# A hybrid recurrent trunk on one core: the SSD's first token piece moved in between the RWKV key steps

## The chip, the cores and the metric

The kernel runs on one core of a Trainium2 chip. The metric is the device time of one execution in microseconds, the median of three runs.

## The reference

The reference is a trunk of two layers over one sequence of 1024 tokens, 1024 wide, in float32. Layer 0 mixes with gated DeltaNet and GLA, layer 1 (the "odd" one) with Mamba-2 SSD and RWKV-7; a squared-ReLU MLP follows each. Only the odd mixer matters here:

```python
z, xbc, dt_raw, pd = _split(h @ w_in, ODD_SPLITS)      # 512, 1024, 8, 1792 columns
xbc = silu(conv(xbc)); dt = softplus(dt_raw + dt_bias)
yc = ssd_chunked(xs, dt, -exp(a_log), b_in, c_in)
yc = rmsnorm((yc + xs * d_skip) * silu(z))
r, k, v, xw, xa, xg = token_shift_mix(pd)              # split of the last 1792 columns
yd = rwkv7_scan(r, decay, k, v, -kk, kk * a)           # 8 heads, state 64 x 64
yd = (groupnorm(yd) + bonus) * g
return concat([yc, yd]) @ w_out
```

## The kernel before

**Products.** Every projection is made in three matmuls per tile: operands are split into a high and a low part (`whi`, `wlo` of the weights, two `hn` tiles of the activations), and high x high, high x low and low x high are added up. `piece` loads a block of weights with SyncE's queue into `wst`, casts it to `whi` on ScalarE and subtracts on VectorE for `wlo`. `feature_tiles` makes 128 features by 512 tokens (24 matmuls of 128x512 per tile). `token_piece` makes 128 tokens by `width` features, four token tiles per half of the sequence. The piece of z and the time steps dt has width 264 (256 columns of z, 8 of dt): 8 x 24 = 192 matmuls of 128x264.

**What sets the order.** The program is one Python pass that emits instructions; a tile scheduler then places them on the engines by priority. Work beside the projections comes in two ways. Closures that an eviction leaves (`later`) stand in `pend`; they are run at the end of a tile (`run_pending(n)`), or, while `spread` is set, a quarter of them after every second k. Background tasks (`spawn`) advance by `step`; `tick(w)` counts columns in units of 512, and every 7 of these are one step in the odd mixer. A 128x264 matmul counts 264/512.

**The odd mixer.** `odd` projects for two groups of four RWKV heads. For each pair p it makes key and receptance tiles (`keys_receptance(p)`), whose closures compute norms, row factors, Gram products (`grams`, tile `G`) and transposed updates, and then values. After both pairs of a group it flushes the closures, stores N of all 16 chunks to DRAM (`d_Nr`), and `inverse(g)` inverts the triangles of the whole group on VectorE, 60 instructions on tile `NL`, and stores them to `d_Ur`. A chunk of the scan loads these into `hh`. After group 1 (g = 0) the scan is spawned (`rwkv`, class "c", a delay of 16 steps) and `spread` is set. The scan runs 32 chunks in order, 16 of group 1 and 16 of group 2, three steps to a chunk, and each chunk's matmuls come as `T` and `Z` (part of the inverse), `uv`, `w`, `Q` (the state) and `r`. While it runs, the rest of the projections fills TensorE: the keys of group 2 (g = 1), the z piece, the SSD's convolved features (`feats`, whose taps are `cy` and `th` on VectorE) and the second z piece. Chunk 14 waits in the program until `begun` holds group 2, that is until the flush behind its key steps. After that come `posts` (group norm, gating and the store to `d_o`), the SSD scan (`ssd_scan`, eight chunks per group, each stores `y` to `d_o`), and `tail`, which reads `d_o` back (`ol`) and makes the output projection (`wst<-in_odd_w_out`, `pd`).

Group 2's key steps are the loop `for p in (2 * g, 2 * g + 1)` with g = 1; z's evictions are `z_evac(0, True)` (gate to `d_z`, time steps to `dtr`); `scalars()` behind it reads `dtr`.

Of the kernel before, what the change touches and what calls it, by code (L numbers as in the profile page):

```python
# [39 lines left out]
class Trunk:  # L40
# [223 lines left out]
    def token_piece(self, cols, width, hnT, evac, halves=(0, 1), mid=None, w=None):  # L264

        w = w or self.token_weights(cols, width)
        for half in halves:
            if half and mid is not None:
                mid()
            hh, hl = hnT[half]  # L270
            for tt in range(4):
                n = len(self.pend)
                sl = slice(tt * 128, tt * 128 + 128)
                ps = self.pd()[:, 0:width]
                for k in range(8):
                    hi, lo = (t[:, k % 2, :] for t in w[k // 2])
                    for j, (wt, x) in enumerate(((hi, hh), (lo, hh), (hi, hl))):
                        self.mm(ps, x[:, k, sl], wt, k + j == 0, k + j == 9)
                        self.tick(width / 512)
                with self.urgent():  # L280
                    evac(half * 4 + tt, ps)
                self.run_pending(n)
# [734 lines left out]
    def odd(self, hnT, d_o, tail):  # L1017
        nc, io, tc = self.nc, self.io, self.tc
        gp = nc.gpsimd
        W = io["odd_w_in"][0]  # L1020
        with ExitStack() as ctx:
# [183 lines left out]
            def values(p):  # L1205
                def v_evac(half, ps):
                    y = mixed(self.s2("my"), half, ps, 8 + p)

                    def turned():
                        pv = self.transpose4(y)  # L1210
                        vt = self.s2("vt")
                        self.cp(vt, pv)
                        self.store(d_v[half * 512:half * 512 + 512, p * 128:p * 128 + 128].rearrange("(c p) d -> p c d", p=128),
                                   vt.rearrange("p (c d) -> p c d", c=4))
                    self.later(turned)
                self.feature_tile(W, 2568 + p * 128, hnT, v_evac)


            def z_evac(c0, gates):
                def f(t, ps):  # L1220
                    if gates:
                        self.vcp(dtr[:, t, :], ps[:, 256:264])
                    self.gate2(ps[:, 0:256], d_z[t * 128:t * 128 + 128, c0:c0 + 256])
                return f

            def xbc_evac(ft):
                def f(half, ps):
                    y = self.conv_silu2(half, ps, self.s_cw, ft, keep, bias=self.s_cb[:, 0, ft:ft + 1])
                    if ft >= 4:
                        kind, gg = (ft - 4) // 2, ft % 2  # L1230
                        self.store(d_bc[half * 4:half * 4 + 4, :, gg, kind, :].rearrange("c f t -> f c t"), y.rearrange("p (c t) -> p c t", c=4))

                    def turned():
                        pt = self.transpose4(y)
                        xt = self.s2("xt")
                        self.cp(xt, pt)
                        dst = d_x[:, ft * 128:ft * 128 + 128] if ft < 4 else d_b[:, (ft - 4) * 128:(ft - 4) * 128 + 128]
                        self.store(dst[half * 512:half * 512 + 512].rearrange("(c p) d -> p c d", p=128), xt.rearrange("p (c d) -> p c d", c=4))
                    if ft < 6:
                        self.later(turned)  # L1240
                return f
# [8 lines left out]
            def inverse(g):  # L1250
                lane = lambda d: d[g].rearrange("k b q x n -> (k b q x) n")
                self.lanes_inverse(lane(d_N), lane(d_U), 128, P)
# [72 lines left out]
            def rwkv():  # L1325

                order = [(g, c) for g in range(2) for c in range(16)]
                own = [[] for _ in order]
                pres = [pre(g, c, own[16 * g + c]) for g, c in order]

                def ahead(i):
                    if i < 32:
                        next(pres[i])

                ahead(0)
                ahead(1)
                ahead(0)
                for _ in pres[0]:
                    yield
                ahead(1)  # L1340
                for i, (g, c) in enumerate(order):
                    while i == 14 and 1 not in begun:
                        yield
                    ahead(i + 2)
                    parts = [chain(g, c, *own[i])] + pres[i + 1:i + 2]
                    for _ in range(3):
                        for p in parts:
                            next(p, None)
                        yield
                    ahead(i + 2)  # L1350
                    if c % 2:
                        scanned.add((g, c // 2))
# [138 lines left out]
            def posts():  # L1491
                for g in range(2):
                    for t in range(8):
                        while (g, t) not in scanned:
                            yield
                        post_p(g, t)
                        yield

            def feats(*fts):
                for ft in fts:  # L1500
                    self.feature_tile(W, 512 + ft * 128, hnT, xbc_evac(ft))

            for g in range(2):
                for p in (2 * g, 2 * g + 1):
                    keys_receptance(p)
                values(2 * g)
                self.flush()
                inverse(g)
                values(2 * g + 1)
                if g == 0:  # L1510
                    self.spawn(rwkv(), "c", 1, 16)
                    self.spread = True
# [7 lines left out]
            gnb = self.bc_row(post_pool, io["rwkv_gn_b"][0], 512, "gnb")  # L1520
            self.scope(ctx, "p", half=1, ldh=5, sm=5)
            self.spawn(posts(), "p", 4, 12)
            self.token_piece([(W, 0, 256), (W, 1536, 8)], 264, hnT, z_evac(0, True))
            with self.core("s"):
                scalars()
            for g in range(2):
# [593 lines left out]
```

## Time and profile before

| | |
|---|---|
| median of three runs | 2557.88 us (2552.94 to 2570.62) |
| profiled execution | 2559.73 us |
| its span | 2557.9 us |
| mean granted clock of TensorE | 0.986 |
| TensorE (PE) busy | 97% |
| weight loads (PEld) | 81% |
| VectorE (DVE) | 64% |
| ScalarE (ACT) | 44% |
| GpSimd (POOL) | 21% |

The profile is one execution, and its own time is 1.85 us above the median of the runs. The odd mixer's projections of group 2 lie at about 1375 to 1519 us, the z piece at 1520 to 1572, the SSD's features up to about 1730, and the end of the SSD scan with the first products of the output projection at 1789 to 1840.

### The profile page before, as it was taken

What the parts mean: (1) busy time and instruction counts of PE and PEld (TensorE: products, weight loads), DVE (VectorE), ACT (ScalarE), POOL (GpSimd) and SP (SyncE); (2) the same over time, 40 slices, a digit from 0 to 9 for tenths busy, and PEclk for the clock granted to TensorE, in tenths of its full rate; (3) what the DMA queues carried; (4) which work ended last, traced back from release to release, by engine and by line L of the source; (5) the groups of instructions that cost most, each with busy time, mean ns of one, the idle gap of its engine ahead of it and who ended that gap; (6) DMA issues with size and microseconds to landing.
All of it is one profiled execution on the core that took longest, in us unless ns stands there. A gap on an engine that the chain in (4) does not pass through costs nothing. (4 is left out here: it accounts for less than half of the span.)

```text
span 2557.9 us, 39479 instructions
## 1 busy us (share of the span) xinstructions
PE 2491.4 (97%) x14230; PEld 2079.6 (81%) x14230; DVE 1645.1 (64%) x2865; ACT 1135.3 (44%) x2139; POOL 541.4 (21%) x546
## 2 busy tenths in 40 slices
PE   7999999999999999999999999999899999999998
PEld 6788898997777788888777788888897778788887
DVE  6677443446587765668366558777657677757476
ACT  5732344336544454333443333444536544533343
POOL 2020123301344300001032202344212443200001
PEclk9999999999999999999999799999999999999999
DMA  4556545644766677566235356666645766677474
GB/s 143 152 152 190 160 140 165 222 141 153 218 231 221 227 268 262 202 254 207 91 112 163 118 161 190 192 187 203 221 149 174 228 217 232 210 275 281 175 265 150
DMA packets 447908, 492.59 MB, mean 193 GB/s; under 512 B 56177, under 2 KB 302178, under 8 KB 447714
## 3 DMA queue, kind: packets, MB, share of 16 engines
q1 hardware_dynamic: 447714, 490.08, 59.3%
q8 instruction: 113, 1.85, 0.3%
q14 instruction: 81, 0.66, 0.1%
HBM read 344.69 MB, written 145.28 MB: 192 GB/s over the span
## 5 line engine op out<-in xcount | busy, mean ns | idle before, releaser
L162 PE MATMUL pd<-hn,whi 128*128 128x512 f32 x1216 | 413.5, 414 | 1.2 <-DVE cy L185 1.1
L162 PE MATMUL pd<-whi,hn 128*128 128x256 f32 (+2 forms) x2048 | 394.0, 288 | 9.4 <-ACT hn L169 4.1
L162 PEld LDWEIGHTS pd<-whi,hn 128*128 128x128 f32 x2048 | 321.8, 190 | 15.5 <-ACT hn L172 4.4
L162 PE MATMUL pd<-wlo,hn 128*128 128x256 f32 (+2 forms) x1024 | 294.9, 288 | 0.6 <-DVE f L182 0.3
L162 PEld LDWEIGHTS pd<-hn,whi 128*128 128x128 f32 x1216 | 225.9, 191 | 54.9 <-issue 8.0
L1864 PE MATMUL pm<-hn,hn 128*128 128x512 f32 x1152 | 263.3, 389 | 0.0
L1864 PEld LDWEIGHTS pm<-hn,hn 128*128 128x128 f32 x1152 | 216.1, 188 | 45.6 <-DVE x L178 0.6
L162 PE MATMUL pd<-hn,wlo 128*128 128x512 f32 x608 | 249.4, 410 | 0.2 <-DVE wlo L178 0.2
L172 ACT CAST hn<-sr 128x1024 fp32r<-128x1024 f32 x104 | 108.9, 1047 | 268.4 <-PE pm L1864 99.3
L178 DVE TENSOR_TENSOR hn<-sr,hn 128x1024 fp32r<-128x1024 f32 x104 | 128.0, 1231 | 113.8 <-ACT hn L172 113.3
L162 PEld LDWEIGHTS pd<-wlo,hn 128*128 128x128 f32 x1024 | 194.4, 190 | 2.7 <-DVE wlo L178 1.2
L189 POOL TENSOR_TENSOR rs<-rs,mhalf 128x1 f32<-128x1 f32 x40 | 24.4, 610 | 769.8 <-DVE rs L178 519.0
L178 DVE TENSOR_TENSOR wlo<-wst,whi 128x512 fp32r<-128x512 f32 (+2 forms) x172 | 125.8, 736 | 90.8 <-ACT whi L172 83.9
L172 ACT CAST whi<-wst 128x512 fp32r<-128x512 f32 (+2 forms) x172 | 106.4, 620 | 175.1 <-PE pd L162 127.5
L1864 PE MATMUL pd<-hn,hn 128*128 128x512 f32 x720 | 182.7, 389 | 0.0
L1864 PE MATMUL pt<-hn,hn 128*128 128x512 f32 x720 | 182.7, 389 | 0.0
L1551 PE MATMUL pm<-rf,whi 128*128 128x512 f32 x512 | 162.8, 399 | 11.0 <-DVE h L178 10.9
L1551 PE MATMUL pm<-hn,whi 128*128 128x512 f32 x512 | 162.4, 398 | 1.8 <-ACT whi L172 1.2
L1864 PEld LDWEIGHTS pt<-hn,hn 128*128 128x128 f32 x720 | 135.1, 188 | 28.1
L1864 PEld LDWEIGHTS pd<-hn,hn 128*128 128x128 f32 x720 | 135.1, 188 | 28.1
L162 PEld LDWEIGHTS pd<-hn,wlo 128*128 128x128 f32 x608 | 116.1, 191 | 25.9 <-issue 1.6
L1551 PEld LDWEIGHTS pm<-rf,whi 128*128 128x128 f32 x512 | 96.9, 191 | 37.0 <-issue 10.3
(439 smaller groups left out, 4922.8 us busy)
## 6 DMA issues: line engine op xcount, KB each, us to landing
w<-in_mlp_w_dram SPq DMA_DIRECT2D x140, 512.0 KB
sr<-d_s SPq DMA_DIRECT2D x104, 512.0 KB
hh<-in_mlp_w_dram SPq DMA_DIRECT2D x64, 512.0 KB
d_s<-s SPq DMA_DIRECT2D x128, 256.0 KB
d_s<-x SPq DMA_DIRECT2D x64, 256.0 KB
hh<-d_rec SPq DMA_DIRECT2D x32, 512.0 KB
wst<-in_even_w_in_dram SPq DMA_DIRECT2D x56, 256.0 KB
wst<-in_odd_w_in_dram SPq DMA_DIRECT2D x52, 256.0 KB
```

The lines of the kernel that those rows point to most:

```text
L162: self.nc.tensor.matmul(out=out, lhsT=lhsT, rhs=rhs, start=start, stop=stop)
L172: self.nc.scalar.copy(out=out, in_=in_)
L178: (eng or self.nc.vector).tensor_tensor(out=out, in0=a, in1=b, op=op)
L189: self.nc.gpsimd.tensor_tensor(out=out, in0=in_, in1=self.mhalf.broadcast_to(list(in_.shape)), op=ALU.pow)
L1551: self.nc.tensor.matmul(out=ps, lhsT=wt[l][:, k, sl], rhs=x[r][:, k, :], start=start and k + j == 0, stop=k + j == n + 1, skip_group_check ...
L1864: self.nc.tensor.matmul(out=ps[tt], lhsT=l[x][:, k, sl], rhs=r[y][:, k, :], start=new and b + k + q == 0, stop=k + q == 5, skip_group_chec ...
```

## The change

The z piece moves from behind the flush of group 2 to between its key steps: tokens of the first half ahead of `keys_receptance(2)`, tokens of the second half ahead of `keys_receptance(3)`. Each call loads and splits the piece's weights itself. `token_piece` gets the spreading of closures that `feature_tiles` has. Nothing else is different.

```diff
@@ token_piece
                 n = len(self.pend)
+                each = -(-n // 4) if self.spread else 0
                 sl = slice(tt * 128, tt * 128 + 128)
                 ps = self.pd()[:, 0:width]
                 for k in range(8):
...
                         self.tick(width / 512)
+                    if k % 2:
+                        now = min(n, each)
+                        self.run_pending(now)
+                        n -= now
                 with self.urgent():
                     evac(half * 4 + tt, ps)
                 self.run_pending(n)
@@ odd
+            def z_early(half):
+                self.token_piece([(W, 0, 256), (W, 1536, 8)], 264, hnT, z_evac(0, True), halves=(half,))
+
             for g in range(2):
                 for p in (2 * g, 2 * g + 1):
+                    if g:
+                        z_early(p - 2)
                     keys_receptance(p)
...
             self.spawn(posts(), "p", 4, 12)
-            self.token_piece([(W, 0, 256), (W, 1536, 8)], 264, hnT, z_evac(0, True))
             with self.core("s"):
                 scalars()
```

**TensorE at the scan's start.** The scan's first chunks stand among the first matmuls of group 2. `pd` is the projection's accumulator, `pm` the scan's. Before, they stand among matmuls of 128x512:

```order
L162 MATMUL pd_2316_13451<-hn_1983_11772,whi_2260_13221 128x512
L162 MATMUL pm_2279_13286<-T_2277_13283,hh_2273_13271 32x32 x4
L162 MATMUL pd_2316_13451<-hn_1984_11773,whi_2260_13221 128x512
L162 MATMUL pd_2316_13451<-hn_1983_11772,wlo_2261_13222 128x512
L162 MATMUL pd_2316_13451<-hn_1983_11772,whi_2260_13221 128x512
L162 MATMUL pm_2289_13320<-hh_2273_13271,Z_2278_13284 32x32 x4
L162 MATMUL pm_2293_13349<-uv_2274_13275,hh_2273_13271 64x64 x4
```

and in the changed kernel among the z matmuls of 128x264:

```order
L162 MATMUL pm_2286_13378<-T_2282_13369,hh_2264_13295 32x32 x4
L162 MATMUL pd_2308_13456<-whi_2303_13445,hn_1983_11772 128x264
L162 MATMUL pd_2308_13456<-wlo_2304_13446,hn_1983_11772 128x264
L162 MATMUL pd_2308_13456<-whi_2303_13445,hn_1984_11773 128x264
L162 MATMUL pd_2308_13456<-whi_2306_13452,hn_1983_11772 128x264
L162 MATMUL pm_2291_13402<-w_2281_13363,hh_2262_13289 64x64 x4
L162 MATMUL pm_2292_13408<-hh_2264_13295,Z_2283_13370 32x32 x4
```

The z piece now lies here, and the key steps of group 2 lie later in the scan by as many steps.

**SyncE where the scan reaches group 2.** `d_Ur<-NL` stores the inverse of group 2; `hh_2654` before and `hh_2652` after are the loads of chunk 16, its first chunk. Before, the store stands here, with group 1's loads behind it and chunk 16's load 25 rows behind the store (not in this piece):

```order
L157 DMA d_Ur_11854<-NL_2458_14100 128x1024
L157 DMA d_z_11850<-th_2574_14772 128x256
L157 DMA d_y_11847<-w_2555_14647 64x256
L157 DMA uv_2579_14788<-d_rv_11845 64x256
L157 DMA hh_2601_14910<-d_Ur_11854 32x4x32
```

In the changed kernel:

```order
L157 DMA d_Ur_11854<-NL_2560_14644 128x1024
L157 DMA wst_3022_16664<-in_odd_w_in_dram 128x4x128
L157 DMA pg_2785_15694<-d_g_11846 128x256
L157 DMA d_o1_11837<-py_2739_15521 128x256
L157 DMA hh_2652_15129<-d_Ur_11854 32x4x32 x2
L157 DMA hh_2677_15237<-d_Ur_11854 32x4x32 x2
L157 DMA hh_2695_15325<-d_Ur_11854 32x4x32 x2
```

The loads of chunks 16, 17 and 18 have moved up to the store.

**SyncE in the tail.** `wst<-in_odd_w_out` are the weights of the output projection, `d_o1<-y` the stores of the SSD chunks (`y_3406` chunk 6, `y_3428` chunk 7 of the second SSD group in the changed kernel). Before, the weights stand here, far ahead of the last chunks:

```order
L157 DMA hh_3453_18395<-d_h_95 128x1024
L157 DMA wst_3456_18401<-in_odd_w_out_dram 128x2x256
L157 DMA wst_3459_18407<-in_odd_w_out_dram 128x2x256
L157 DMA wst_3462_18413<-in_odd_w_out_dram 128x2x256
L157 DMA d_y_11847<-w_3144_17135 64x256
L157 DMA d_o1_11837<-y_3093_16938 128x256
L157 DMA wst_3465_18419<-in_odd_w_out_dram 128x2x256
```

In the changed kernel:

```order
L157 DMA d_o1_11837<-y_3406_18194 128x256
L157 DMA ol_3445_18331<-d_o1_11837 128x512
L157 DMA ol_3446_18333<-d_o1_11837 128x512
L157 DMA wst_3468_18429<-in_odd_w_out_dram 128x2x256
L157 DMA ol_3453_18351<-d_o1_11837 128x512
L157 DMA ol_3454_18353<-d_o1_11837 128x512
L157 DMA d_o1_11837<-y_3428_18255 128x256
L157 DMA wst_3471_18435<-in_odd_w_out_dram 128x2x256
L157 DMA wst_3474_18441<-in_odd_w_out_dram 128x2x256
L157 DMA wst_3477_18447<-in_odd_w_out_dram 128x2x256
```

The projection's loads have moved behind the stores of the last two chunks. On TensorE in the same place, the projection's first matmuls (`pd_3468` before, `pd_3480` after) stood among the SSD chunks' small ones (`xdt,E`, `bc`, `xdd,sb`, `sS,bc`; `ident,ol` are the tail's transposes):

```order
L162 MATMUL pm_3348_18005<-xdt_3324_17889,E_3308_17811 128x64 x4
L162 MATMUL pm_3358_18036<-bc_3329_17928 128x128
L162 MATMUL pd_3468_18425<-whi_3457_18403,hn_3294_17746 128x256
L162 MATMUL pd_3468_18425<-wlo_3458_18404,hn_3294_17746 128x256
L162 MATMUL pm_3360_18041<-xdd_3326_17891,sb_3307_17807 128x256
L162 MATMUL pm_3362_18046<-sS_3336_17950,bc_3305_17805 128x256
```

In the changed kernel the first of them has 30 rows of small matmuls right ahead of it, of which these are the last:

```order
L162 MATMUL pm_3444_18325<-xdt_3427_18254,E_3413_18209 128x64 x4
L162 MATMUL pm_3447_18335<-sS_3435_18286,bc_3410_18203 128x256
L166 MATMUL pm_3455_18355<-ident_78,ol_3445_18331 128x128 x4
L166 MATMUL pm_3456_18368<-ident_78,ol_3446_18333 128x128 x4
L162 MATMUL pd_3480_18453<-whi_3469_18431,hn_3292_17726 128x256
```

They have moved from among the chunks to behind the last one.

## Rows read from the trace of the kernel before

**Rows 1.** The page's first lines: span; busy time, share and instructions of each engine.

```profile
span 2557.9 us, 39479 instructions
PE 2491.4 (97%) x14230; PEld 2079.6 (81%) x14230; DVE 1645.1 (64%) x2865; ACT 1135.3 (44%) x2139; POOL 541.4 (21%) x546
```

**Rows 2.** Windows: stretch and length, busy time per engine, granted clock, DMA share, GB/s.

```profile
core 0: us, PE busy (x) PEld busy (x) DVE busy (x) ACT busy (x) POOL busy (x), PEclk, DMA share, GB/s
1424.50:1434.70 10.20, 10.20 (x68) 8.43 (x65) 1.95 (x5) 2.87 (x8) 0.00 (x0) 0.50 0.15 52
1451.80:1472.30 20.50, 20.50 (x77) 15.83 (x77) 7.51 (x14) 4.31 (x9) 5.01 (x4) 0.50 0.30 92
1503.00:1509.80 6.80, 6.80 (x28) 5.81 (x27) 0.04 (x1) 1.57 (x4) 1.34 (x1) 0.50 0.60 193
1519.80:1572.00 52.20, 52.20 (x496) 46.84 (x494) 42.22 (x138) 17.36 (x47) 7.08 (x10) 1.00 0.62 179
1793.10:1800.00 6.90, 4.47 (x15) 3.85 (x16) 5.22 (x14) 5.74 (x19) 4.19 (x7) 0.51 0.58 183
```

**Rows 3.** Timeline of PE: wide matmuls at full clock, then at the lower one.

```profile
start us, us, engine line op out<-in xcount [idle before <-releaser]
1391.04 0.63 PE L162 MATMUL pd<-hn,whi 128*128 128x512 f32 x2
1391.50 0.40 PE L162 MATMUL pd<-hn,wlo 128*128 128x512 f32 x1
1455.45 1.05 PE L162 MATMUL pd<-hn,whi 128*128 128x512 f32 x2
1456.31 0.63 PE L162 MATMUL pd<-hn,wlo 128*128 128x512 f32 x1
```

**Rows 4.** Timeline of PE: the matmuls of one scan chunk, between wide ones.

```profile
1483.32 0.68 PE L162 MATMUL pm<-r,hh 64*64 64x64 f32 x8
1484.29 1.16 PE L162 MATMUL pt<-ar,bk 64*128 64x128 f32 x16
...
1488.41 1.82 PE L162 MATMUL pm<-uv,hh 128*128 128x128 f32 x20
1490.16 0.50 PE L162 MATMUL pd<-hn,whi 128*128 128x512 f32 x1
...
1492.79 0.61 PE L162 MATMUL pm<-Q,hh 128*128 128x128 f32 x4
1493.69 0.50 PE L162 MATMUL pd<-hn,wlo 128*128 128x512 f32 x1
```

**Rows 5.** Timeline of PE: matmuls of the z piece.

```profile
1526.94 0.41 PE L162 MATMUL pd<-whi,hn 128*128 128x264 f32 x2
1527.18 0.28 PE L162 MATMUL pd<-wlo,hn 128*128 128x264 f32 x1
```

**Rows 6.** Lines by form: z weights' splits (1490 to 1545), conv taps (1572 to 1700).

```profile
L178 DVE TENSOR_TENSOR wlo<-wst,whi 128x528 fp32r<-128x528 f32 x2 | 1.4, 709 | 1.3 <-ACT whi L172 1.3
L172 ACT CAST whi<-wst 128x528 fp32r<-128x528 f32 x2 | 1.3, 634 | 0.9 <-PE pd L162 0.9
L185 DVE SCALAR_TENSOR_TENSOR cy<-pd,cols,cy 128x511 f32<-128x511 f32 x11 | 8.2, 742 | 3.1 <-ACT cy L169 3.1
```

**Rows 7.** Tile NL, 1500 to 1600 (count, ns min/median/max, first and last start).

```profile
L178 DVE TENSOR_TENSOR tl<-NL x30: 185/337/543, 1519.6 to 1557.7; 128x30 f32<-128x30 f32 x2, 128x58 f32<-128x58 f32 x2, 128x84 f32<-128x84 f32 x2, 128x108 f32<-128x108 f32 x2
L178 DVE TENSOR_TENSOR NL<-NL,tl x30: 166/345/620, 1520.1 to 1558.4; 128x30 f32<-128x30 f32 x2, 128x58 f32<-128x58 f32 x2, 128x84 f32<-128x84 f32 x2, 128x108 f32<-128x108 f32 x2
L157 SPq DMA_DIRECT2D d_Ur<-NL x1: 320/320/320, 1558.7 to 1558.7; - x1
```

**Rows 8.** Timeline of SyncE's queue: chunk 16's loads of the inverse.

```profile
1579.66 0.80 SPq L157 DMA_DIRECT2D hh<-d_Ur  x2
```

**Rows 9.** Timeline of SyncE's queue in the tail: projection's weights, last stores.

```profile
1750.79 1.45 SPq L157 DMA_DIRECT2D wst<-in_odd_w_out_dram  x3
1798.43 0.32 SPq L157 DMA_DIRECT2D d_o<-y  x1
1827.00 0.34 SPq L157 DMA_DIRECT2D d_o<-y  x1
1831.97 0.32 SPq L157 DMA_DIRECT2D d_o<-y  x1
```

**Rows 10.** Windows of PE's matmuls into pd alone in the tail.

```profile
1788.90:1832.00 43.10, 24.14 (x152) 0.92 0.74 232
```

## The prediction

> **What bounds the kernel now.** I read the page's head first: TensorE (PE) is busy for 2491.4 of 2557.9 us [rows 1]. No other engine comes near, so a change can save time in two ways only: by filling the little idle time of PE, or by getting its matmuls done at a higher clock. The windows of granted clock come next, over the odd mixer's projections, because that is where the change works. They show something that the share of busy time hides: PE is busy throughout, yet three stretches of the group 2 key steps run at 0.50 of the clock (10.2, 20.5 and 6.8 us, 37.5 us together), while the z piece behind them runs at 1.00 [rows 2]. The timeline gives the price of that. A wide matmul (128x512) starts 0.23 us after the one before it at full clock (1391.04 to 1391.50 is two of them), and 0.43 us at the lower level (1455.45 to 1456.31) [rows 3]. So of low-clock time a share of 1 - 0.23/0.43 = 0.465 is lost, 17.4 us of the 37.5. That is all the key steps could give.
>
> The scan of RWKV is the other actor. One chunk of it costs PE about 3.62 us: 0.97 for r and Z, 1.75 for the three uv products, 0.90 for Q and T [rows 4]. A chunk is spread over three steps of seven wide matmuls, thus 21 x 0.233 + 3.62 = 8.5 us at full clock.
>
> **The change part by part.**
>
> *The matmuls of z.* The same 192 matmuls of 128x264 run once before and once after, 0.12 us each [rows 5] (1526.94 to 1527.18 holds two): 23 us on both sides, net 0.
>
> *Weights loaded and split twice.* Each call loads four pieces, so there are four more casts (0.634 us on ScalarE) and four more subtractions (0.709 us on VectorE) [rows 6], with eight more loads on SyncE. That is 2.5 us and 2.8 us. VectorE has 7.51 us of work in the 20.50 us stretch [rows 2], so I cost both at nothing; if that cover is gone it is +2.8.
>
> *Clock in the key steps.* The order shows z matmuls taking the place of wide ones around the same small scan matmuls; the scan still starts 16 steps after its spawn, only that it now starts among z matmuls. Between -17.4 (no low stretch left) and +17 (as much again, since the closures of the key rows are now run among smaller matmuls) no row decides. The low stretches lie at the scan's start and among the grams of the key rows, and both occur after the change too, so I take 0.
>
> *Where the 14 steps went.* 192 x 264/512 columns at seven to a step are 14 steps. Before, the z piece lay behind the flush, over the inversion of group 2: the inversion's rows run from 1519.6 to 1558.4 on VectorE, its result is stored at 1558.7 [rows 7], and chunk 16 (the first of group 2) loads it at 1579.66 [rows 8], after the loads of chunks 14 and 15 in the same queue. That is 21.0 us of slack. Afterwards, the scan has run 14 steps (14/3 x 8.5 = 39.7 us) more when the inversion begins. And the inversion takes longer: VectorE's order has 86 other instructions among its 60, where 50 were, with 14 conv taps and 4 gate products of 0.74 us among the added ones, and four more splits of 0.709 [rows 6]. That makes 18 x 0.74 + 4 x 0.709 = 16 us on top of the 38.8. Chunk 16 is therefore late by 39.7 - 21.0 + 16 = 35 us. The order agrees: the store of the inverse and the loads of chunks 16, 17 and 18 stand within seven rows of SyncE, and chunk 16's T stands behind 93 wide matmuls with no scan among them. PE has these matmuls to run, so the lateness is no idle time by itself. What it leaves is a catch-up: seven chunks among only 55 wide matmuls, where before 147 (7 x 21) went with them. In time that is 7 x 3.62 + 55 x 0.23 = 38 us, PE mostly on 32- and 64-wide matmuls. The nearest rows for such a mix are the low stretches of the key steps; the longest is 20.50 us at 0.50 with 77 PE entries, all of it busy [rows 2]. I take one stretch like it: 20.5 x 0.465 = +9.5. Bounds: 0 (full clock), and the whole 38 us at the lower level, 38 x (0.43/0.23 - 1) = +33.
>
> The Trainium skill (TensorE: Matmul & The Clock Gate, What's actually happening) has the clock lowered for an idle PE and full for a busy one. By that rule a busy catch-up would cost no clock, and the sum would be 9.5 less; this trace does not bear it out, since PE is busy for 20.50 of 20.50 us at 0.50.
>
> *The tail of the mixer.* Behind the second z piece come the SSD scan and the first half of the output projection. Before, three of the projection's weight loads are issued together at 1750.79 [rows 9], so its matmuls stand ready as filler: 152 of them run between 1788.90 and 1832.00 [rows 10], among the last SSD chunks whose results are stored at 1798.43, 1827.00 and 1831.97 [rows 9]. Afterwards SyncE's order has the first of these loads behind the store of SSD chunk 6 and the other three behind that of chunk 7, the last one. So PE runs 30 rows of small matmuls without a single wide one, and all 152 come behind them: 152 x 0.12 = +18.2 us that had been hidden. Against it, SSD chunks without filler go faster: the last five intervals between stores (1798.43 to 1831.97) take 33.5 us; at the fastest of these, 1827.00 to 1831.97 or 5.0 us, they take 25, which gives 8.5 back. Net +9.7. Bounds: 0 (SyncE reaches the loads earlier than its rows suggest, or the small chunks run much faster) and +21.4 (nothing given back, and 6.9 us of the products at the lower level, as PE had at 1793.10 to 1800.00 [rows 2], +3.2).
>
> **Sum.** 0 + 0 + 0 + 9.5 + 9.7 = +19.2 us. Against the profiled execution of 2559.73 us that is 2578.9. That execution lies 1.85 us above the median of the three runs shown, 2557.88, so the forecast is 2577.
>
> **Rivals.**
>
> *A, faster: the interleaving pays.* The z matmuls in the key steps fill PE so that no low stretch is left there (-17.4), and catch-up and tail cost nothing: 2559.73 - 17.4 - 1.85 = 2541. For it: the z piece, matmuls of 0.12 us among scan chunks, now runs at 1.00 [rows 2, 5]. Against it: PE is already busy for every us of the low stretches, so filler doesn't raise its busy share. It decides if the key steps show fewer than about 10 us at 0.50. The Trainium skill (Perfetto Trace Analysis, Optimization Strategy) says that interleaving stretches with different busiest engines may help; here PE is the busiest in both, and no row shows a second regime.
>
> *B, no change.* PE has the same work at 97% busy, the lateness of chunk 16 is covered by the 93 wide matmuls, and the tail's loads aren't as late as their rows. Net 0: 2558.
>
> *C, slower.* The catch-up runs at the lower level for all of its 38 us (+33) and the tail loses the full 18.2: 2559.73 + 51.2 - 1.85 = 2609. It decides when the low stretch behind chunk 16's T lasts over 40 us. For it: the scan's small matmuls run at 0.50 in three stretches. Against it: the z piece runs at 1.00 for 52.20 us with scan chunks in it too [rows 2].
>
> *D, the tail alone.* The catch-up runs at full clock: 2559.73 + 9.7 - 1.85 = 2568.
>
> **How the numbers follow.** Chances: the forecast 0.40 (2570 to 2592, from its terms' nearer bounds), A 0.12, B 0.20, C 0.22, D 0.06. About 1%, 25.6 us, is what a measurement of this kernel can tell from no change; it lies at 2532.3 and 2583.5. Faster than that is only the lower quarter of A, 0.03. Slower are C and a third of the forecast's range, 0.22 + 0.13 = 0.35. The rest, 0.62, is within 1%. The range of 2548 to 2604 leaves out most of A (0.10) and the upper half of C (0.10).
>
> **What would show it.** (1) Windows of the key steps: the z matmuls at 0.12 us, and the time at 0.50 near 37 us; under 10 us is A. (2) VectorE's inversion of group 2 near 55 us rather than 39, and SyncE's loads for chunk 16 directly behind its store. (3) Behind chunk 16's T a stretch at 0.50 of some 20 us; none means D or B, 40 and more C. (4) In the tail, the loads of the output projection's weights at the last SSD stores, the first product behind the last chunk, and intervals of about 5 us between stores. The forecast is wrong if PE idles waiting for chunk 16, which I've put at 0 because the wide matmuls stand ahead of it in PE's order, or if the products run among the chunks after all.

## The result, and the profile after

The changed kernel took 2593.58 us (median of four runs, 2586.79 to 2599.52) against 2557.33 for the kernel before in the same comparison: a ratio of 1.0147, interval 1.0113 to 1.0181. Timed again in a later comparison (e5) it came to 1.0123, 1.0094 to 1.0151. It is slower by 28 to 36 us. The forecast was +19, to 2577, with a range of 2548 to 2604.

The page's head after: the span grew by 38.2 us, and PE's busy time by only 8.2.

```profile
span 2596.1 us, 39483 instructions
PE 2499.6 (96%) x14230; PEld 2081.3 (80%) x14230; DVE 1650.5 (64%) x2869; ACT 1136.5 (44%) x2143; POOL 547.7 (21%) x546
```

So 30 of the 38 us are idle time of PE. The rest is that the same 14230 matmuls keep PE busy for longer, which is the clock. To see where, I cut both executions at the same three matmuls. The wide matmuls stand in one order among themselves in all kernels of this text, so the n-th from the end is the same piece of work. The stretches are: key steps (with z in both kernels), features, tail (second z piece, end of the SSD scan, output projection, up to an early wide matmul of the MLP), and what is left of the span. The windows of the kernel before:

```profile
1363.00:1578.60 215.60, 213.44 (x1464) 172.04 (x1463) 132.61 (x354) 74.72 (x164) 39.63 (x36) 0.91 0.50 148
1578.60:1748.50 169.90, 169.72 (x1295) 136.20 (x1294) 133.01 (x336) 82.29 (x211) 61.30 (x84) 1.00 0.68 194
1748.50:1930.70 182.20, 170.76 (x1318) 160.79 (x1318) 112.19 (x257) 84.60 (x218) 47.28 (x70) 0.97 0.57 181
1930.70:2557.90 627.20, 611.94 (x2665) 498.56 (x2663) 428.41 (x506) 286.56 (x421) 121.04 (x84) 0.99 0.66 224
```

and those of the changed kernel:

```profile
1364.30:1568.70 204.40, 199.66 (x1464) 160.41 (x1463) 120.92 (x312) 75.54 (x165) 28.28 (x23) 0.97 0.52 152
1568.70:1758.30 189.60, 182.12 (x1308) 145.53 (x1308) 138.91 (x355) 78.17 (x204) 63.87 (x83) 0.93 0.59 165
1758.30:1967.50 209.20, 182.26 (x1305) 166.84 (x1304) 125.47 (x284) 88.30 (x229) 58.68 (x84) 0.89 0.54 174
1967.50:2596.10 628.60, 611.33 (x2665) 497.12 (x2663) 427.19 (x506) 286.81 (x421) 120.71 (x84) 1.00 0.66 223
```

Length less PE's busy time is idle time; the column PEclk is the mean granted clock. The key steps are 11.2 us shorter (clock 0.91 to 0.97), the features 19.7 longer (7.5 us idle, clock 1.00 to 0.93), the tail 27.0 longer (idle 11.4 to 26.9, clock 0.97 to 0.89), the end 1.4 longer. The start, 1363.0 against 1364.3, adds 1.3. Together 38.2.

Three places of the changed kernel answer to the steps of the prediction. The inversion of group 2, which answers to [rows 7]:

```profile
L178 DVE TENSOR_TENSOR tl<-NL x30: 183/333/483, 1551.7 to 1603.1; 128x30 f32<-128x30 f32 x2, 128x58 f32<-128x58 f32 x2, 128x84 f32<-128x84 f32 x2, 128x108 f32<-128x108 f32 x2
L178 DVE TENSOR_TENSOR NL<-NL,tl x30: 164/346/648, 1551.9 to 1604.2; 128x30 f32<-128x30 f32 x2, 128x58 f32<-128x58 f32 x2, 128x84 f32<-128x84 f32 x2, 128x108 f32<-128x108 f32 x2
L157 SPq DMA_DIRECT2D d_Ur<-NL x1: 367/367/367, 1605.8 to 1605.8; - x1
```

From the first of its instructions to its store it takes 54.1 us, where it took 39.1. PE's timeline at chunk 16, with the idle time ahead of an instruction in brackets:

```profile
1611.91 0.63 PE L162 MATMUL pd<-hn,whi 128*128 128x512 f32 x2
1614.66 0.43 PE L162 MATMUL pm<-T,hh 32*32 32x32 f32 x8 [2.12 <-DVE m L182]
1615.03 0.67 PE L162 MATMUL pm<-r,hh 64*64 64x64 f32 x8
1615.63 0.51 PE L162 MATMUL pd<-hn,wlo 128*128 128x512 f32 x1
```

and the windows of what follows it and of the longest low stretch of the tail:

```profile
1616.00:1639.90 23.90, 23.90 (x147) 18.87 (x146) 11.04 (x28) 6.25 (x18) 3.08 (x4) 0.50 0.38 105
1824.20:1854.90 30.70, 19.95 (x77) 16.19 (x77) 19.62 (x52) 14.83 (x45) 9.63 (x14) 0.50 0.72 237
```

SyncE's queue in the tail, which answers to [rows 9], its stores to `d_o` and loads of the output projection's weights alone: `d_o<-y` are the SSD's stores, `d_o<-py` those of the posts.

```profile
1805.25 0.32 SPq L157 DMA_DIRECT2D d_o<-py  x1
1811.58 0.32 SPq L157 DMA_DIRECT2D d_o<-y  x1
1816.97 0.32 SPq L157 DMA_DIRECT2D d_o<-py  x1
1821.59 0.32 SPq L157 DMA_DIRECT2D d_o<-y  x1
1830.13 0.32 SPq L157 DMA_DIRECT2D d_o<-py  x1
1832.37 0.32 SPq L157 DMA_DIRECT2D d_o<-y  x1
1839.21 0.32 SPq L157 DMA_DIRECT2D d_o<-y  x1
1841.74 0.32 SPq L157 DMA_DIRECT2D d_o<-y  x1
1843.06 0.44 SPq L157 DMA_DIRECT2D wst<-in_odd_w_out_dram  x1
1848.38 0.32 SPq L157 DMA_DIRECT2D d_o<-y  x1
1848.76 1.74 SPq L157 DMA_DIRECT2D wst<-in_odd_w_out_dram  x3
```

The weights come with the last store, as the order said, and behind the last store the tail has 1967.5 - 1848.38 = 119.1 us still to go, against 1930.7 - 1831.97 = 98.7 before. What that does to PE shows from the end of the second z piece to the last SSD store (before) and the first product (changed), two windows of all of PE's matmuls:

```profile
1788.80:1832.00 43.20, 36.68 (x267) 33.92 (x265) 30.75 (x82) 25.42 (x77) 15.44 (x25) 0.92 0.74 232
1802.40:1849.40 47.00, 27.87 (x117) 20.79 (x115) 31.74 (x84) 21.52 (x70) 23.56 (x35) 0.62 0.70 221
```

Before, some 150 of the 267 matmuls are products of the output projection. The changed kernel has the others without them, takes 3.8 us longer, idles for 19.1 us and runs at 0.62 of the clock. The posts are what I hadn't reckoned with: six of them store after the start of the second z piece (1758.3), where two did before.

### The profile page after: what moved, and what is told of

Read it like the earlier page. It is cut to its first block, busy times and chain, and to the rows that moved or that the text cites. A ratio compares the mean times of both kernels' runs of the same rounds, so it can differ in the third digit from the quotient of the medians.

```text
span 2596.1 us, 39483 instructions
## 1 busy us (share of the span) xinstructions
PE 2499.6 (96%) x14230; PEld 2081.3 (80%) x14230; DVE 1650.5 (64%) x2869; ACT 1136.5 (44%) x2143; POOL 547.7 (21%) x546
## 5 line engine op out<-in xcount | busy, mean ns | idle before, releaser
L172 ACT CAST hn<-sr 128x1024 fp32r<-128x1024 f32 x104 | 108.9, 1047 | 270.1 <-PE pm L1873 103.9
L178 DVE TENSOR_TENSOR wlo<-wst,whi 128x512 fp32r<-128x512 f32 (+2 forms) x176 | 130.5, 747 | 98.6 <-ACT whi L172 90.1
L162 PEld LDWEIGHTS pd<-hn,wlo 128*128 128x128 f32 x608 | 115.1, 189 | 26.1 <-issue 1.3
```

What stands on the lines that cost most here:

```text
L162: self.nc.tensor.matmul(out=out, lhsT=lhsT, rhs=rhs, start=start, stop=stop)
L172: self.nc.scalar.copy(out=out, in_=in_)
L178: (eng or self.nc.vector).tensor_tensor(out=out, in0=a, in1=b, op=op)
```

## The experiments

The theory after the result had three places: key steps (a gain by the clock), a catch-up behind chunk 16, and a tail that lost its filler. The first rival: only the scan's lateness counts, and everything in the tail follows from that.

Each row below gives the ratio to the kernel before with its interval, and of the profile the features and the tail as length / PE idle / mean clock.

| kernel | ratio | features | tail |
|---|---|---|---|
| before | 1 | 169.9 / 0.2 / 1.00 | 182.2 / 11.4 / 0.97 |
| changed | 1.0147 (1.0113 to 1.0181) | 189.6 / 7.5 / 0.93 | 209.2 / 26.9 / 0.89 |
| e1 scan 7 steps later | 1.0127 (1.0082 to 1.0172) | 173.4 / 2.6 / 1.00 | 218.8 / 26.2 / 0.90 |
| e2 weights early | 1.0136 (1.0090 to 1.0181) | 182.2 / 6.2 / 0.96 | 203.9 / 25.0 / 0.92 |
| e3 both | 1.0105 (1.0061 to 1.0149) | 174.1 / 3.5 / 1.00 | 209.6 / 23.4 / 0.95 |
| e4 first half only | 1.0103 (1.0043 to 1.0162) | 176.3 / 4.5 / 1.00 | 204.3 / 24.0 / 0.91 |
| e5 changed again | 1.0123 (1.0094 to 1.0151) | 187.4 / 6.7 / 0.94 | 208.9 / 26.1 / 0.89 |
| e6 posts early | 1.0118 (1.0088 to 1.0148) | 183.5 / 6.9 / 0.95 | 204.9 / 22.4 / 0.90 |
| e7 before, posts late | 1.0023 (0.9998 to 1.0048) | 171.1 / 1.0 / 1.00 | 186.7 / 16.3 / 0.97 |
| e8 posts and weights early | 1.0128 (1.0084 to 1.0171) | 206.9 / 8.4 / 0.84 | 192.9 / 18.2 / 0.96 |
| e9 before, weights held | 1.0103 (1.0070 to 1.0135) | 170.6 / 1.0 / 1.00 | 212.7 / 29.0 / 0.90 |
| e10 half, repaired | 1.0088 (1.0058 to 1.0119) | 191.0 / 10.3 / 0.96 | 191.8 / 18.3 / 0.96 |
| e11 no spreading | 1.0126 (1.0093 to 1.0158) | 187.4 / 7.2 / 0.94 | 206.4 / 26.1 / 0.90 |
| e12 before, scan earlier | 1.0040 (1.0012 to 1.0067) | 168.4 / 2.3 / 1.00 | 178.3 / 13.8 / 0.97 |

**The catch-up alone.** e1 lets the scan start seven steps later, so that chunk 16 isn't late.

```diff
-                    self.spawn(rwkv(), "c", 1, 16)
+                    self.spawn(rwkv(), "c", 1, 23)
```

> The changed kernel with one number altered: the scan is spawned with a delay of 23 steps, not 16, so that group 2's chunks come due seven steps later and stand among wide matmuls again (128 wide ones beside chunks 16 to 22, where the changed kernel has 48). Theory 'three places' (key steps about -11 us, catch-up behind chunk 16 about +16, tail about +22): the catch-up goes, the tail stays, 2594 - 16 = 2578 us (2572 to 2584), with no stretch at 0.50 behind chunk 16's T and idle and low clock in the tail as in the changed kernel. Rival 'late scan': the tail suffers because the scan and all behind it end late; a scan that starts 7 steps later makes it worse, 2594 us or more.

```profile
1558.90:1732.30 173.40, 170.77 (x1307) 137.49 (x1306) 137.88 (x355) 79.27 (x207) 65.53 (x86) 1.00 0.66 186
1732.30:1951.10 218.80, 192.65 (x1414) 177.06 (x1414) 126.59 (x296) 92.63 (x237) 60.76 (x83) 0.90 0.53 173
```

For the features the theory held: they take 173.4 us at 1.00, 16 less than in the changed kernel. Its 2582.77 us lie inside the 2572 to 2584 expected, but only because all runs of that set were faster: against its own runs of before (2545.55) it is +37 us, where +20 was meant. The tail's row tells why: 1414 PE instructions stand in it, where the changed kernel has 1305. Some hundred scan matmuls have moved behind the features, and the tail is 9.6 us longer. Both theories were half right: the features lose their catch-up, and the later scan costs in the tail. In the times e1 can't be told from the changed kernel: its interval overlaps with those of both timings (1.0147 and 1.0123).

**The weights alone, and both.** e2 makes the first four weight loads of the output projection ahead of the SSD scan's last steps (the four make up one block of 256 columns); e3 adds the later scan.

```diff
             self.spawn(tail.feed(1, 4, ready), "s", 1, 0)
+            tail.w0 = self.token_weights([(tail.W, 0, 256)], 256)
             while len(self.oT) < 2 or (0, 1, 7) not in done:
...
-            K.token_piece([(self.W, c0, 256)], 256, K.oT, evac, halves=(half,))
+            K.token_piece([(self.W, c0, 256)], 256, K.oT, evac, halves=(half,), w=getattr(self, 'w0', None) if not (c0 or half) else None)
```

> The changed kernel with the first four weight pieces of the output projection loaded and split ahead of the last steps of the SSD scan in the program, not behind the loads of the residual tiles. Theory 'three places': the products are filler again among the SSD chunks, the tail's +22 us goes, the catch-up stays: 2594 - 22 = 2572 us (2565 to 2580), and the first product runs before the last four SSD stores. Rival 'late scan': the SSD chunks themselves are late, products among them change nothing but the order: 2588 us or more.

> Both edits, the scan's delay of 23 and the early weights. Theory 'three places': only the gain of the key steps is left, 2594 - 16 - 22 = 2556 us (2546 to 2562). Rival 'late scan': 2585 us or more, since the later scan pushes the SSD further back. If the two terms share one cause, the sum saves less than 38 us.

Both missed. In e2 the tail is 5.3 us shorter than in the changed kernel, not 22: one block of weights is 96 products, or 11.5 us of filler, and the blocks behind it came no sooner. The trace splits the 5.3: 89 products run before the last SSD store, so what comes behind that store is 10.2 us shorter (108.9 where the changed kernel has 119.1), but with products among them the chunks reach the store 4.9 us later (95.0 us from the start of the tail, where it was 90.1). e3 has features at 1.00 and a tail like the changed kernel's. The two repairs together gave 1.0105, 5 to 11 us less than the changed kernel's 1.0123 to 1.0147, where 38 were expected. So putting one block of loads back doesn't undo the tail's loss.

**Half the tokens.** e4 moves only the first half's tokens; the second half's stay behind the flush.

```diff
-                    if g:
-                        z_early(p - 2)
+                    if p == 2:
+                        z_early(0)
                     keys_receptance(p)
...
+            self.token_piece([(W, 0, 256), (W, 1536, 8)], 264, hnT, z_evac(0, True), halves=(1,))
```

> Only the first half's tokens of z are moved ahead of the third pair's key steps; the second half's stay behind the flush. In the order 141 wide matmuls stand beside chunks 16 to 22, and 30 small rows stand ahead of the first product as in the changed kernel. Theory 'three places': no catch-up, half the key steps' gain, the tail's +22: 2557 - 5 + 22 = 2574 us (2568 to 2582). A rival in which the loss goes with the number of tokens moved (half of +36): 2575 us, but then with half of each loss in the trace: a catch-up at 0.50 of about 12 us and a tail of half the idle time.

Its time (1.0103) doesn't tell the two apart: +30 us in medians of that set is more than the +17 and +18 that they expected. The profile does. The features run at 1.00, so the catch-up doesn't come by halves. The tail takes 204.3 us, 82% of the changed kernel's loss. For the places this bears the theory out, and it speaks against a loss in proportion to the tokens moved.

**The posts.** e5 is the changed kernel again. e6 moves its posts ten steps forward, e7 delays those of the kernel before by 14.

```diff
-            self.spawn(posts(), "p", 4, 12)
+            self.spawn(posts(), "p", 4, 2)
```

> The changed kernel itself, as the yardstick for the others of this set on the same chip: +36 us or 1.0147 of before. Every theory expects the same.

> The changed kernel with one number altered: the posts (group norm, gating, store of RWKV's tiles) are spawned with a delay of 2 steps, not 12, so that three of them instead of six stand behind the weights of the second z piece in SyncE's order. Theory 'posts': the SSD chunks of the tail didn't get faster without filler because six posts run among them on VectorE, ScalarE and GpSimd; with three, the last SSD store comes some 8 us (5 to 14) sooner after the start of the second z piece than the 87.8 us of the changed kernel, and the time is 8 us less, 1.0115 of before. Rival 'chain': the SSD chunks have a pace of their own and the posts fill gaps: 87.8 us and 1.0147 as before.

> The kernel before with one number altered: the posts are spawned with a delay of 26 steps, not 12, so that they come as late as in the changed kernel (six behind the second z piece's weights), while z and the scan stay where they were and the products remain filler. Theory 'posts': the last SSD store comes 5 to 10 us later than the 82.1 us of before, part of which the products fill: +3 to +8 us, 1.001 to 1.003. Rival 'chain': no change, 1.000.

e6 shortens the tail by some 4 us against e5 (idle 26.1 to 22.4), and e7 lengthens that of before by 4.5 (idle 11.4 to 16.3). The posts are part of it, by one profile each about 4 us, which for e6 is half of what was expected. In e6 3.6 of the 4.0 us lie behind the last SSD store (115.9 against 119.5), so it doesn't show that the chunks themselves got faster. In the times e6 is no better than e5 beyond their intervals, and e7 lies at 1.0023, where no change is not excluded either.

**Posts and weights.**

```diff
-            self.spawn(posts(), "p", 4, 12)
+            self.spawn(posts(), "p", 4, 0)
...                                            (and the weights as in e2)
```

> The changed kernel with posts at a delay of 0 and the first four weight pieces of the output projection ahead of the SSD scan's last steps. By the order 70 products stand ahead of the last SSD chunk's product, where the changed kernel has none and the kernel before 86. Theory 'posts and products': -8 for the posts and 70 x 0.12 = -8 for the products, 1.0147 - 0.006 = 1.008 of before. Rival: only one of the two is real, 1.011; or neither, 1.0147.

The time missed (1.0128). The tail did what was expected: 192.9 us, 16 less than the changed kernel's.

```profile
1568.50:1775.40 206.90, 198.46 (x1320) 159.58 (x1319) 146.16 (x379) 79.58 (x208) 71.02 (x92) 0.84 0.56 159
1775.40:1968.30 192.90, 174.66 (x1305) 162.62 (x1304) 117.04 (x261) 86.50 (x223) 50.20 (x74) 0.96 0.57 182
```

The features paid for it: 206.9 us at a clock of 0.84. Posts that leave the tail go to the features, where the catch-up is. That this execution's profile is a bad draw of the clock can't be excluded, as its time was 2598.86 and the six runs spread from 2573 to 2604.

**The tail alone, in the kernel before.** e9 leaves z, scan and posts as they were and holds the first four weight loads of the output projection back until the last SSD store.

```diff
+        self.hold = []
...
         v = st[:, 0:nk * width].rearrange("p (k c) -> p k c", k=nk)
+        if self.hold:
+            self.load(st[:, 0:256], self.hold.pop())
...
+            self.hold = [d_o[896:1024, 256:512]] * 4
             with self.core("s"):
                 tail.products(0, self.big)
```

> The kernel before with one thing added: each of the first four weight tiles of the output projection is first loaded from the rows that the last SSD chunk stores, so that their true load can't be issued until that store is done. z, scan and posts stay as before. Theory 'filler': the products leave the SSD chunks as in the changed kernel, from the last SSD store to the first matmul of the MLP is about 105 us (86 before), PE runs thin among the chunks and gets the lower clock there; the stretch from the end of the features to the MLP is 182 us before, 209 in the changed kernel, and about 204 here (the posts' share of some 4 us stays out): +20 us, 1.008 of before (1.006 to 1.010). Rival 'late posts and scan': the products' place costs little by itself, 1.002 or less. The key steps of this kernel are those of before, instruction by instruction: if their low-clock stretches (37.5 us in the profile of before) are a property of the order, they show again; if they are one execution's, they differ.

```profile
1363.00:1564.30 201.30, 199.14 (x1462) 161.04 (x1461) 133.04 (x354) 74.24 (x163) 39.00 (x36) 0.98 0.53 158
1564.30:1734.90 170.60, 169.59 (x1296) 136.34 (x1294) 133.03 (x336) 82.58 (x210) 61.90 (x84) 1.00 0.68 193
1734.90:1947.60 212.70, 183.74 (x1318) 168.44 (x1318) 114.63 (x257) 85.21 (x219) 47.85 (x70) 0.90 0.49 157
```

This is the plainest of the runs. One cause alone turns the tail of before (182.2 us, 11.4 idle, 0.97) into one like the changed kernel's (212.7, 29.0, 0.90), and costs 28.5 us by the medians of its set (2579.39 against 2550.86), more than the 20 that were expected. Its weights come 5.5 us behind the last store, where the changed kernel's come 5.3 ahead of it to 0.4 behind, so it overstates that kernel's case. By how much PE's first product says: it starts at 1823.25, 8.9 us behind the last store, and in the changed kernel at 1849.43, 1.1 behind. By this estimate some 8 of the 28.5 us belong to the way of holding the loads back (each tile is first filled from `d_o`), and about 20 are left, near what was expected. The SSD's stores in it:

```profile
1783.13 0.32 SPq L158 DMA_DIRECT2D d_o<-y  x1
...
1814.39 0.32 SPq L158 DMA_DIRECT2D d_o<-y  x1
1819.89 0.38 SPq L158 DMA_DIRECT2D wst<-in_odd_w_out_dram  x1
```

The five intervals up to the last one take 31.3 us. Without filler the chunks go faster by 2.2 us than the 33.5 of before, no more.

All traces together show the same. The stretch from the last SSD store to the end of the tail goes with how many products run before that store. With 150 to 158 of them (before, e7, e10, e12) it takes 98.7 to 100.1 us, with 88 to 96 (e2, e3, e8) 106.4 to 111.2, and with none to 7 (changed, e1, e4, e5, e6, e11) 115.9 to 120.8. e9, with none and a late start, takes 133.2.

e9 answers a second question. Its key steps are those of the kernel before, instruction by instruction on PE, VectorE and ScalarE; in e7 six matmuls and some of the posts' work on VectorE stand elsewhere. They took 201.3 and 201.1 us at 0.98, where the profile of before shows 215.6 at 0.91. (Both windows start a few matmuls late; cut at the same matmul as before, they are 201.8 and 202.3.) So most of the 37.5 us at the lower clock belonged to that one execution, or to the chip that it ran on.

**Half, with all repairs.** e10 moves the first half's tokens only, with weights early and posts at period 3 and delay 8.

> A version meant to keep what is good in the change: only the first half's tokens of z are moved ahead, the second half's stay behind the flush; the posts come with period 3 and delay 8 (two of them behind the second z piece's weights), and the first four weight pieces of the output projection come ahead of the SSD scan's last steps. By the order 114 wide matmuls stand beside chunks 16 to 22, and 92 products ahead of the last SSD chunk's. Theory 'three places': no catch-up, a tail like before's (182 to 188 us), and at most some us of gain in the key steps: 1.001 of before (0.997 to 1.004). Rival 'lost filler': whatever z is moved ahead is missed at the end, so half of the loss stays: 1.006 or more.

The time is the one that the rival 'lost filler' expected: 1.0088. The tail (191.8 us) is nearly mended, the features are not (191.0, of which 10.3 idle). Why they idle more than in e4, whose features take 176.3, was not settled; the posts at the shorter period are the one difference in the program that falls there, and in the order 114 wide matmuls stand beside chunks 16 to 22 where e4 has 141.

**Without the spreading.** e11 undoes the first edit.

```diff
-                each = -(-n // 4) if self.spread else 0
+                each = 0
```

> The changed kernel without its first edit: the z piece's closures are run at the end of a token tile, not a quarter after every second k. Neither the catch-up nor the tail hangs on it: 1.012 of before (1.010 to 1.015), as for the changed kernel. If the spreading is what keeps the clock up in the key steps, their low stretches grow (10.2 us in the changed kernel) and the time with them.

As expected: 1.0126, and all three stretches as in the changed kernel. The spreading neither gives nor takes anything that these runs can show.

**The other direction.** e12 is the kernel before with the scan seven steps sooner and the posts denser.

```diff
-                    self.spawn(rwkv(), "c", 1, 16)
+                    self.spawn(rwkv(), "c", 1, 9)
...
-            self.spawn(posts(), "p", 4, 12)
+            self.spawn(posts(), "p", 3, 8)
```

> The kernel before, z left behind the flush, with two numbers altered the other way: the scan is spawned with a delay of 9 steps, not 16, and the posts with period 3 and delay 8, not 4 and 12. Chunk 16's slack of 21 us pays for the seven steps (20 us), in the order 147 wide matmuls stand beside chunks 16 to 22 as before, and two posts instead of three and 90 products stand in the tail. Theory 'filler behind the inverse is what the tail lives on': what ends earlier leaves a tail with less idle time than the 11.4 us of before; no catch-up: 0.9975 of before (0.994 to 1.000), the stretch from the features' end to the MLP 174 to 181 us where before has 182. Rival: the tail's 182 us are bound by the SSD chunks' own chain, and nothing changes (1.000); or chunk 16 is late again and a stretch at 0.50 comes behind its T (1.005).

```profile
1361.50:1581.80 220.30, 214.63 (x1578) 172.98 (x1577) 140.25 (x371) 78.41 (x177) 38.39 (x36) 0.95 0.51 151
1581.80:1750.20 168.40, 166.10 (x1252) 133.83 (x1251) 135.57 (x339) 81.33 (x207) 66.14 (x88) 1.00 0.68 197
1750.20:1928.50 178.30, 164.46 (x1250) 156.03 (x1248) 105.53 (x238) 81.43 (x210) 44.50 (x66) 0.97 0.54 175
```

The tail's length came out as expected (178.3), its idle time (13.8 us, not under 11.4) and the time (1.0040, slower) did not. The scan's matmuls that left features and tail stand in the key steps now (1578 PE instructions, where 1464 were). These grew by 4.7 us over the profile of before, less than the 5.4 that the other two lost, but by some 18 over the key steps of e9 and e7. Part of that is clock (0.95 against 0.98), and one profile doesn't say how much would come again.

No kernel of these beats the one before.

## Why the prediction was right in sign and short in size

*Moved matmuls and second loading of the weights: 0.* This held within what the profiles can tell. The key steps have 1464 PE instructions before and after. Against e9's and e7's key steps (201.8 and 202.3 us, cut at the same matmul) the changed kernel's 204.4 is 2 us more, and PE idles 4.7 us in them where it idled 2.2. The same cut gives 201.5 to 204.2 in e2, e5, e6 and e8, which share the changed kernel's key steps, so no cost of the extra splits is shown.

*Clock in the key steps: 0, bounds -17.4 to +17.* As an effect of the change the 0 was right; as a term counted from that profile it was not. In the two profiles compared, the key steps get 11.2 us shorter, most of it clock, and 10.2 us at 0.50 are left in them where the prediction's sign asked for near 37 and rival A for under 10. But most of the 37.5 us of [rows 2] don't belong to the order of instructions: e9 has the same order at 0.98. There was little there to be won.

*Inversion 55 us, PE not idle at chunk 16.* The inversion held closely: 54.1 us were measured, and the loads of chunk 16 come 5.5 us behind the store. The waiting did not. PE idles 2.12 us ahead of chunk 16's T, which the prediction had put at 0 and named as a sign of being wrong. It is a small time, but it may count for more than itself. In the five profiles with a low stretch right behind this T (changed, e2, e5, e8, e11) PE had idled for 1.5 to 2.1 us just ahead of it. In e6, where the same six loads come together and PE did not idle there, the clock stayed up:

```profile
1607.00:1640.00 33.00, 32.86 (x307) 26.31 (x305) 26.15 (x72) 18.96 (x51) 9.79 (x12) 1.00 0.55 157
```

No run varied this idle time alone, so that it brings the low clock on isn't shown; the three low stretches of the key steps in [rows 2] had none ahead of them.

*Catch-up: +9.5 (0 to +33).* The low stretch is 23.9 us where 20.5 was taken, and 147 PE instructions run in it with PE busy throughout. That is 11.1 us by the same 0.465. The Trainium skill (TensorE: Matmul & The Clock Gate, What's actually happening) has the clock lowered for an idle PE and full for a busy one. The 2.12 us idle ahead of T fit the first half of that; the stretch itself, 23.90 of 23.90 us busy at 0.50, doesn't agree with the second. The features grew by 19.7 all the same: 7.3 us of idle time came with it, which the prediction had at 0. Less than half of that is at chunk 16 (2.12 us ahead of its T, 1.39 a little earlier); the rest is spread over the features up to 1740. e1 shows the whole as a unit: without the lateness the features take 173.4.

*Tail: +9.7 (0 to +21.4).* Here the sum failed, and beyond its upper bound: +27.0. The first half was right. What comes behind the last SSD store grew by 20.4 us, where 152 products were priced at 18.2. The second half, 8.5 us given back by chunks that run without filler, was wrong: the last five intervals take 36.8 us (1811.58 to 1848.38) where 33.5 stood before and 25 were forecast. Taking the fastest of five intervals for all of them was the error: instead of -8.5 they cost +3.3. The last 3.3 us of the 27.0 come ahead of these intervals. e9, whose posts come when they did before, gives back 2.2 us in the five, which points to chunks that mostly wait for their own chain. So the small matmuls leave PE idle (26.9 us in the tail, 15.5 more) and at 0.89 of its clock. For the 6.6 us ahead of the last store the late posts are the likeliest cause: e7, which delays them alone, reaches that store 3.1 us later than before. Its time doesn't show it clear of noise. The order had shown them ten and more steps later, and I gave that no price.

*The sum.* That the time fell into the stated range is in part luck. The two priced places came to 19.7 + 27.0 = 46.7 us where 19.2 were forecast, and 11.2 of that came back only because the profile they are counted from had unusually slow key steps.

*What the terms have in common.* Tail and catch-up were costed as two places. e1, e8, e10 and e12 suggest that they draw on one supply: what is taken out of one of them turns up in the other, or in the key steps. That isn't shown, as e8 and e12 rest on one profile each whose clock may be chance, and in e4 both places are shorter than in the changed kernel. Behind the inversion of group 2 lies a fixed amount of chain work (16 scan chunks, the posts, 16 SSD chunks), and it needs wide or z matmuls beside it. The change took 192 x 0.12 = 23 us of these away from there and put them where PE was busy anyway. The loss came out near that number, and a little above. That it follows from the number is not shown, and e4 speaks against it: it moves half of these matmuls and loses 1.0103.

*Rivals.* A (2541, by its sum 2540) and B (2558) fell with the time. C (2609) was wrong in its cause, the catch-up at the lower level for 38 us (23.9 were measured), though the time fell midway between it and the forecast, a little nearer to C. D's catch-up without a clock loss did not occur in the changed kernel.

## What to carry to other kernels

When independent matmuls are moved out of a place, ask first what small work they stood beside there, and count how much filler is left for it up to the next point where everything has to be finished; a busy share of 97% says nothing on that. Read the order of every queue that the move shifts by as many steps, and price each piece of work that ends up in a tail, the posts here as well as the weight loads. Don't let the fastest of a few intervals stand for all of them. And before a stretch of low clock is priced from one profile, look whether a second execution has it too.

## What the runs showed of the hardware

How long PE runs at the lower clock while it is busy differs between executions. One and the same sequence of instructions ran its key steps in 215.6 us at 0.91 in one execution (before) and in 201.3 at 0.98 in another (e9). The runs of the kernel before spread from 2539.62 to 2570.62 over the comparisons, and a lone profile's low stretches can't be taken for a property of the kernel.

What repeats is the low clock in the features of the kernels that have the catch-up (mean 0.84 to 0.96). In five of the six profiles a low stretch of 13.7 to 23.9 us begins right behind chunk 16's T, ahead of which PE had idled. In the sixth, e6, it didn't idle there; its low stretch lies some 108 us later (1717.1 to 1734.2), behind an idle time of 1.75 us. In e1, e3, e4, e7, e9 and e12, which don't have the catch-up, the features run at 1.00. Only e10 has no such catch-up by its order and still 0.96.
